# Second blocks of stick-breaking weights turned by VectorE, weights' low halves on GpSimd, v through DRAM, and the rotary product in another pool

## The chip, the cores and the metric

The kernel runs on one core of a Trainium2 chip. The metric is the device time of one execution in microseconds; lower is better. The time of a kernel is the median of several runs.

## The reference, cut to what matters

One layer of an encoder trunk over 1024 frames and 16 meta tokens (T = 1040 rows, 1024 features). `u` is the normalised input; one projection gives queries, keys, values and gates of two kinds of attention; both are gated and projected back.

```python
proj = jnp.einsum('bld,dc->blc', u, w_in)
sb_q, sb_k, sb_v, sb_g, df_q, df_k, df_v, df_g = jnp.split(proj, idx, axis=-1)

# stick-breaking attention: 8 heads of 64, strictly causal
z = einsum(q, k) * scale
log_beta = log_sigmoid(z)
log_keep = where(strict, log_sigmoid(-z), 0)
stick = reversed cumulative sum of log_keep
w = where(strict, exp(log_beta + stick), 0)
o = einsum(w, v)

# differential attention: 4 heads, rotary on q and k
p = softmax(where(mask, einsum(q, k) * scale, -1e30))
a = p[:, :, 0] - lam * p[:, :, 1]
o = rmsnorm(einsum(a, v), subln_g) * (1 - lambda_init)

mix = concat([sb_o * silu(sb_g), df_o * silu(df_g)])
h = h + einsum(mix, w_out);  y = rmsnorm(h, final_norm_gain)
```

## The kernel before

The sequence is stored in reverse, so a query block b of 128 rows sees the keys from its own place to the end: NB - b key tiles and 16 remaining columns. Work is cut into eight groups. Groups 0 to 3 are stick-breaking, two heads each (`sb_attention`); groups 4 to 7 are differential, one head each (`df_steps`). `build` puts the attention of group gi beside the projection of group gi + 1 with `weave`, which advances whichever of the two generators is behind by estimated TensorE time; the last two groups are woven with the output projection. What `weave` emits is then put in order for each engine by the framework's planner, which uses estimated durations (TC_OPTS, L922). Each engine runs its own queue strictly in that order. All DMAs that matter here are issued from SyncE's queue, also in order.

A projection unit (`proj`, L162) is one of v, q, k, g of a group: its weights come in two halves by `w_half` (L140). Each half is loaded into `wraw` (two buffers), rounded by ScalarE to a high part `wh` (L146), and VectorE subtracts for the low part `wl` (L147); `wh` and `wl` have three buffers each. Three matmuls (L157 to L159) use high times high, high times low and low times high, into one of two PSUM banks "mm". `ORDER` (L912) lists the units of each group: for groups 1 to 6 q, v, the remainder of v (r), k, g.

`sb_weights` (L512) makes the weights of one block of one head: scores on TensorE (L508, L509), a mask on VectorE (L520), two sigmoids on ScalarE (L521, L522), a running product on VectorE (scan, L525), and a multiplication (L527); a corner of it is copied by GpSimd (L528). `sb_transpose` (L531) turns it one step later, tile by tile of 128 keys. For even blocks of four tiles or more (8, 6 and 4 tiles, blocks 0, 2 and 4), as long as the rotary tables are not loaded, `turn` (L251) does it: VectorE transposes 32x32 squares into a spare tile (the buffers of the rotary tables `cosr` and `sinr`, two in all), four DMAs write that to DRAM (L260), and one DMA loads it back into place (L262). All other blocks go through TensorE (L551) and ScalarE (L552). `sb_pv` (L556) multiplies a pair of blocks with v (L574). `df_constants` loads the rotary tables when q of group 4 begins, at the start of project(4), which runs beside the attention of group 3; so group 3 uses TensorE alone.

`make_v` (L264) turns v of groups 1 to 6: VectorE transposes 32x32 squares, and 16 DMAs of 32 KB move them into place (L283). `evac_rope` (L202) empties PSUM for the rotary q and k: a product with the cosine (L209), two half products with the sine into a tile `t2` (L211) from the pool `a4` (tag "be", four buffers, that the attention uses for its weights), and an add on GpSimd (L212). The pool `tp` (tag "t", three buffers) holds the projections' results, the low part of q and v's turned tile.

Of the kernel before, what the change touches and what calls it, by code (L numbers as in the profile page):

```python
# [19 lines left out]
F32 = mybir.dt.float32  # L20
# [5 lines left out]
P = 128  # L26
D = 1024
SEQ = 1024
NMETA = 16
T = SEQ + NMETA  # L30
NB = SEQ // P
# [12 lines left out]
def chunks(width):  # L44
    if width <= 512:
        return [(0, width)]
    if width <= 1024:
        h = (width // 4) * 2
        return [(0, h), (h, width - h)]
    return list(CH_K)  # L50


class Build:
    def __init__(self, tc, es, i, out, mix_dram, turn_dram):
        self.tc, self.nc, self.es, self.i = tc, tc.nc, es, i
        self.out, self.mix_dram, self.turn_dram = out, mix_dram, turn_dram
        self.n = 0

        self.nu, self.rotary = 0, False

    def name(self, s):
        self.n += 1
# [77 lines left out]
    def w_half(self, u, h, copy=None, room=None):  # L140

        nc = self.nc
        raw = self.tl(self.wp2, [P, 4, P], F32, "wraw")
        nc.sync.dma_start(out=raw, in_=self.i["w_in"][u, :, 4 * h:4 * h + 4, :])
        hi, lo = room or (self.tl(self.wp3, [P, 4, P], F32R, n) for n in ("wh", "wl"))
        (copy or nc.scalar.copy)(out=hi, in_=raw)  # L146
        nc.vector.tensor_sub(lo, raw, hi.bitcast(F32))  # L147
        return hi, lo

    def mm3(self, ps, w, kt, c0, cn):  # L150
# [51 lines left out]
    def evac_rope(self, t):  # L202

        nc = self.nc

        def post(ps, c0, cn):
            s = slice(c0, c0 + cn)
            t2 = self.tl(self.a4, [P, T], F32, "be")
            nc.vector.tensor_mul(t[:, s], ps[:, :cn], self.cosr[:, s])  # L209
            for a, b in ((0, 64), (64, 0)):  # L210
                nc.vector.tensor_mul(t2[a:a + 64, :cn], ps[b:b + 64, :cn], self.sinr[a:a + 64, s])  # L211
            nc.gpsimd.tensor_add(t[:, s], t[:, s], t2[:, :cn])  # L212
        return post
# [34 lines left out]
                self.move(a[r + n:r + 2 * n], a[r:r + n])  # L248
        st["kh"], st["kl"] = (ha, hb), (la, lb)

    def turn(self, u, src, dst):  # L251


        nc = self.nc
        n = src.shape[1] // P
        nc.vector.transpose(out=u[:, :n * P].rearrange("p (m t r) -> p t m r", m=4, r=32),
                            in_=src.rearrange("p (t m r) -> p t m r", m=4, r=32))
        d = self.turn_dram[self.nu % 4]
        for a in range(4):
            nc.sync.dma_start(out=d[:, a, :n * 32].rearrange("(m k) c -> k m c", k=32),  # L260
                              in_=u[32 * a:32 * a + 32, :n * P].rearrange("k (m c) -> k m c", m=4))
        nc.sync.dma_start(out=dst, in_=d[:, :, :n * 32].rearrange("p a (t r) -> p a t r", r=32))  # L262

    def make_v(self, t, st, sb, on_pe):  # L264


        nc = self.nc
        v = self.tl(self.a2, [P, NB, P], F32, "v")
        off = NMETA if sb else 0
        if on_pe:  # L270
            for j0 in range(0, NB, 4):
                tr = self.bank("tr")
                for j in range(4):
                    c = off + P * (j0 + j)
                    nc.tensor.transpose(tr[:, j * P:(j + 1) * P], t[:, c:c + P], self.ident)
                nc.scalar.copy(out=v[:, j0:j0 + 4, :], in_=tr)
        else:
            u = self.tl(self.tp, [P, T], F32, "t")[:, :SEQ]
            nc.vector.transpose(out=u, in_=t[:, off:off + SEQ])
            u = u.rearrange("p (t j r) -> p t j r", j=4, r=32)  # L280
            for a in range(0, P, 32):
                for j in range(4):
                    nc.sync.dma_start(out=v[32 * j:32 * j + 32, :, a:a + 32], in_=u[a:a + 32, :, j, :])  # L283
        st["v"] = v
        if sb:
            tc_ = self.tl(self.a3, [P, P], F32, "on")
            nc.gpsimd.tensor_copy(tc_.rearrange("p (b c) -> p b c", c=16),
                                  t[:, :SEQ].rearrange("p (b c) -> p b c", c=P)[:, :, :16])
            st["vrt"] = tc_
        else:  # L290
            st["vrt"] = t[:, SEQ:T]
# [50 lines left out]
    def project(self, gi, st, first=False):  # L342
# [33 lines left out]
        parts = {"v": v, "r": vr, "q": q, "k": k, "g": g}  # L376
        for part in (parts[c] for c in ("vr" if first else ORDER[gi])):
            yield from part()
# [133 lines left out]
    def sb_weights(self, st, hd, b):  # L512
        nc = self.nc
        kw = T - b * P
        beta = self.tl(self.a4, [P, T], F32, "be")
        keep = self.tl(self.a4, [P, T], F32, "be")
        for c0, cn in chunks(kw):
            z = self.qk(st, hd, b, c0, cn)
            if c0 == 0:
                nc.vector.tensor_add(z[:, :P], z[:, :P], self.zmask)  # L520
            nc.scalar.activation(keep[:, c0:c0 + cn], z[:, :cn], AF.Sigmoid, scale=-1.0)  # L521
            nc.scalar.activation(beta[:, c0:c0 + cn], z[:, :cn], AF.Sigmoid)  # L522
            yield 2 * cn * MM_NS
        yield SB_PAD
        nc.vector.tensor_tensor_scan(out=keep[:, :kw], data0=keep[:, :kw], data1=self.zero.to_broadcast([P, kw]),  # L525
                                     initial=1.0, op0=ALU.mult, op1=ALU.add)
        nc.vector.tensor_mul(beta[:, 1:kw], beta[:, 1:kw], keep[:, :kw - 1])  # L527
        nc.gpsimd.tensor_copy(st["wrem"][32 * hd:32 * hd + 16, b], beta[:16, :16])  # L528
        st["w", hd, b] = beta

    def sb_transpose(self, st, hd, b):  # L531

        nc = self.nc
        n = NB - b
        e = b % 2
        w = st.pop(("w", hd, b))
        if e == 0:
            wt = self.tl(self.a2, [P, 2 * NB * P], F32, "wt")
            st["wt", hd] = wt.rearrange("p (e a j r) -> p e a j r", e=2, a=4, r=32)
        wt = st["wt", hd][:, e]  # L540
        if e == 0 and n >= SB_TURN and not self.rotary:
            self.nu += 1
            u = self.tl(self.const, [P, T], F32, ("cosr", "sinr")[self.nu % 2])
            self.turn(u, w[:, NMETA:NMETA + n * P], wt[:, :, e:e + n])
            return
        for m0 in range(0, n, 4):
            mn = min(4, n - m0)
            tr = self.bank("tr")
            for m in range(mn):
                c = NMETA + P * (m0 + m)  # L550
                nc.tensor.transpose(tr[:, m * P:(m + 1) * P], w[:, c:c + P], self.ident)  # L551
            nc.scalar.copy(out=wt[:, :, m0 + e:m0 + e + mn].rearrange("p a m r -> p m a r"),  # L552
                           in_=tr[:, :mn * P].rearrange("p (m a r) -> p m a r", a=4, r=32))
            yield mn * 110
# [354 lines left out]
END_PAD = 3000  # L909
LEAD, CUT, CUT_NS = 5, 8, 22e3  # L910

ORDER = [""] + 6 * ["qvrkg"] + ["qkvrg"]  # L912

SB_TURN = 4

AHEAD = 3
LAST_CUT = [(0, 512), (512, 256), (768, 256)]
# [61 lines left out]
```

## Time and profile before

| | |
|---|---|
| Median of 3 runs | 689.79 us (686.61 to 689.93) |
| The profiled execution | 689.24 us |
| Its span, first to last instruction | 687.4 us |
| TensorE busy | 663.5 us, 97% of the span |
| VectorE busy | 513.2 us, 75% |
| ScalarE busy | 350.8 us, 51% |
| GpSimd busy | 137.0 us, 20% |
| TensorE clock granted, mean | 0.987 |

Busy time is a share of one execution. Matmuls are pipelined and their ends are modelled, so that a busy TensorE can still run below its peak. An engine's idle time is put down to what came last before it went on. PE is TensorE, PEld its weight loads, DVE is VectorE, ACT ScalarE, POOL GpSimd and SPq the queue of SyncE, which issues the DMAs.

### The profile page before, as it was taken

What the parts mean: (1) busy time and instruction counts of PE and PEld (TensorE: products, weight loads), DVE (VectorE), ACT (ScalarE), POOL (GpSimd) and SP (SyncE); (2) the same over time, 40 slices, a digit from 0 to 9 for tenths busy, and PEclk for the clock granted to TensorE, in tenths of its full rate; (3) what the DMA queues carried; (4) which work ended last, traced back from release to release, by engine and by line L of the source; (5) the groups of instructions that cost most, each with busy time, mean ns of one, the idle gap of its engine ahead of it and who ended that gap; (6) DMA issues with size and microseconds to landing.
All of it is one profiled execution on the core that took longest, in us unless ns stands there. A gap on an engine that the chain in (4) does not pass through costs nothing.

```text
span 687.4 us, 11400 instructions
## 1 busy us (share of the span) xinstructions
PE 663.5 (97%) x3908; PEld 577.5 (84%) x3908; DVE 513.2 (75%) x1053; ACT 350.8 (51%) x931; POOL 137.0 (20%) x188
## 2 busy tenths in 40 slices
PE   8999999999979998989999999999999999999996
PEld 7888998798858996779878998899889987888785
DVE  6744998699829985698858785878589687776653
ACT  6513545545534552565544656555655436655642
POOL 0030021122210112040411022202222053011222
PEclk9999999999989999999999999999999999999998
DMA  8215647374645658022352324042504772122322
GB/s 327 93 33 140 171 124 188 87 218 121 144 118 138 165 112 239 16 77 55 72 123 62 74 67 124 32 117 53 124 32 101 201 239 87 63 84 77 105 92 92
DMA packets 76617, 78.83 MB, mean 115 GB/s; under 512 B 32528, under 2 KB 56208, under 8 KB 76560
## 3 DMA queue, kind: packets, MB, share of 16 engines
q1 hardware_dynamic: 76416, 78.10, 41.6%
q8 instruction: 31, 0.51, 0.3%
q14 instruction: 26, 0.21, 0.1%
q10 hardware_dynamic: 144, 0.00, 0.0%
HBM read 41.44 MB, written 14.42 MB: 81 GB/s over the span
## 4 chain that ended last, share of the span: by engine, by line
PE 71%; DVE 10%; DMA 8%; issue 3%; ACT 3%; SPq 3%; POOL 1%; POOLq 0%; DVEq 0%; ACTq 0%
PE mm L157 12%; PE mm L158 12%; PE mm L159 12%; PE mm L756 10%; PE pv L694 4%; PE z L508 4%; PE z L509 4%; PE pv L574 3%; DVE be L525 2%; PE tr L677 2%; DMA wt<-turn_scratch 2%; PE tr L551 2%; DVE be L527 1%; DMA hb<-ha 1%; SPq L283 1%
## 5 line engine op out<-in xcount | busy, mean ns | idle before, releaser
L157 PE MATMUL mm<-xh,wh 128*128 128x346 f32 (+2 forms) x592 | 211.6, 358 | 2.6 <-DVE be L211 2.2
L158 PE MATMUL mm<-xl,wh 128*128 128x346 f32 (+2 forms) x592 | 210.9, 356 | 0.0
L159 PE MATMUL mm<-xh,wl 128*128 128x346 f32 (+2 forms) x592 | 209.9, 355 | 0.0
L157 PEld LDWEIGHTS mm<-xh,wh 128*128 128x128 f32 x592 | 112.3, 190 | 13.3 <-DVE be L211 2.5
L159 PEld LDWEIGHTS mm<-xh,wl 128*128 128x128 f32 x592 | 112.1, 189 | 9.1 <-issue 0.5
L158 PEld LDWEIGHTS mm<-xl,wh 128*128 128x128 f32 x592 | 112.2, 189 | 8.5 <-issue 0.7
L525 DVE TENSOR_TENSOR_SCAN be<-be,zero 128x1040 f32<-128x1040 f32 (+7 forms) x64 | 92.2, 1446 | 16.5 <-ACT be L521 16.4
L521 ACT ACTIVATE be<-z 128x456 f32<-128x456 f32 (+8 forms) x112 | 49.8, 458 | 86.7 <-DVE z L520 51.2
L643 ACT ACTIVATE be<-z,nm 128x346 f32<-128x346 f32 (+8 forms) x112 | 59.9, 540 | 50.4 <-DVE nm L640 34.6
L528 POOL COPY rem<-be 16x16 f32<-16x16 f32 x64 | 34.6, 540 | 192.0 <-DVE be L527 177.0
L633 DVE TENSOR_REDUCE nm<-z 128x1 f32<-128x346 f32 (+8 forms) x112 | 54.6, 502 | 4.7 <-PE z L509 3.6
L522 ACT ACTIVATE be<-z 128x346 f32<-128x346 f32 (+8 forms) x112 | 48.6, 464 | 13.3 <-DVE be L527 12.1
L146 ACT CAST wh<-wraw 128x512 fp32r<-128x512 f32 x58 | 36.2, 626 | 36.6 <-PE mm L158 27.2
L527 DVE TENSOR_TENSOR be<-be,be 128x1039 f32<-128x1039 f32 (+7 forms) x64 | 49.2, 769 | 4.0 <-ACT be L522 0.9
L147 DVE TENSOR_TENSOR wl<-wraw,wh 128x512 fp32r<-128x512 f32 x58 | 40.0, 691 | 10.3 <-ACT wh L146 9.7
L702 POOL TENSOR_TENSOR rr<-rr,mhalf 128x1 f32<-128x1 f32 x32 | 19.7, 616 | 137.8 <-DVE rr L701 98.9
L508 PE MATMUL z<-ha,qa 128*128 128x346 f32 (+8 forms) x112 | 37.9, 344 | 4.2 <-DMA ha<-ha 1.9
L574 PE MATMUL pv<-wt,v 128*64 128x256 f32 (+1 forms) x336 | 37.4, 368 | 4.6 <-DMA wt<-turn_scratch 4.6
L508 PE MATMUL z<-hb,qb 128*128 128x346 f32 (+8 forms) x112 | 38.2, 341 | 0.6 <-ACT be L522 0.3
L552 ACT COPY wt<-tr 128x512 f32<-128x512 f32 (+3 forms) x66 | 28.7, 461 | 19.1 <-PE pv L574 9.5
L694 PEld LDWEIGHTS pv<-v,wt 128*128 128x128 f32 x288 | 36.8, 191 | 1.8
L694 PE MATMUL pv<-v,wt 128*128 128x128 f32 x288 | 38.2, 275 | 0.0
(237 smaller groups left out, 1220.1 us busy)
## 6 DMA issues: line engine op xcount, KB each, us to landing
wraw<-w_in SPq DMA_DIRECT2D x58, 256.0 KB, 3.0
t<-w_out SPq DMA_DIRECT2D x8, 512.0 KB, 4.3
wt<-turn_scratch SPq DMA_DIRECT2D x6, 512.0 KB, 4.4
v<-t SPq DMA_DIRECT2D x96, 32.0 KB, 2.0
mix_scratch<-gate SPq DMA_DIRECT2D x6, 512.0 KB, 4.0
t<-mix_scratch SPq DMA_DIRECT2D x16, 192.0 KB, 2.5
wt<-turn_scratch SPq DMA_DIRECT2D x6, 384.0 KB, 4.2
hb<-ha SPq DMA_DIRECT2D x8, 260.0 KB, 3.9
```

Of the source, the lines that this page charges most:

```text
L157: nc.tensor.matmul(o, hi[:, k, :], xh, start=kt == 0, stop=False)
L158: nc.tensor.matmul(o, hi[:, k, :], xl, start=False, stop=False)
L159: nc.tensor.matmul(o, lo[:, k, :], xh, start=False, stop=kt == KT - 1)
L508: nc.tensor.matmul(z[:, :cn], q, st["kh"][hd][:, s], start=True, stop=False)
L521: nc.scalar.activation(keep[:, c0:c0 + cn], z[:, :cn], AF.Sigmoid, scale=-1.0)
L525: nc.vector.tensor_tensor_scan(out=keep[:, :kw], data0=keep[:, :kw], data1=self.zero.to_broadcast([P, kw]), initial=1.0, op0=ALU.mult, op1 ...
L527: nc.vector.tensor_mul(beta[:, 1:kw], beta[:, 1:kw], keep[:, :kw - 1])
L574: nc.tensor.matmul(pv[r, s], st["v"][:, b + j, r], w, start=p in ends[0], stop=p in ends[1])
L633: nc.vector.tensor_reduce(out=nm[:, comp, j:j + 1], in_=z[:, :cn], op=ALU.max, axis=AX.X, negate=True)
L643: nc.scalar.activation(p[:, c0:c0 + cn], zs[j][:, :cn], AF.Exp, bias=bias, accum_out=sm[:, comp, j:j + 1])
L694: nc.tensor.matmul(po[:, :P], wt[:, m, :], st["v"][:, b + m, :], start=m == 0, stop=False)
L756: self.nc.tensor.matmul(ps[:, :cn], a, b[kt][:, w], start=first and n == 0, stop=last and n == 2)
```

## The change

- `w_half`: the low half of the weights is subtracted by GpSimd instead of VectorE.
- `evac_rope`: the tile `t2` comes from the pool `tp` instead of `a4`.
- `turn` only transposes and writes to DRAM, and returns a function that loads. The first part now runs at the end of `sb_weights`, the load in `sb_transpose`.
- `SB_TURN` is a pair: even blocks of four tiles or more are turned in this way, and now odd blocks of five or more too (7 and 5 tiles, blocks 1 and 3). Eight places in DRAM are used in turn instead of four.
- `make_v`: the 16 direct DMAs become `turn` with four writes and four loads.
- `ORDER`: group 4 projects g first, then q, v, r, k.

```diff
@@ w_half
-        nc.vector.tensor_sub(lo, raw, hi.bitcast(F32))
+        nc.gpsimd.tensor_sub(lo, raw, hi.bitcast(F32))
@@ evac_rope
-            t2 = self.tl(self.a4, [P, T], F32, "be")
+            t2 = self.tl(self.tp, [P, T], F32, "t")
@@ turn
-    def turn(self, u, src, dst):
+    def turn(self, u, src):
...
-        d = self.turn_dram[self.nu % 4]
+        self.nd += 1
+        d = self.turn_dram[self.nd % 8]
         for a in range(4):
             nc.sync.dma_start(out=d[:, a, :n * 32].rearrange("(m k) c -> k m c", k=32),
                               in_=u[32 * a:32 * a + 32, :n * P].rearrange("k (m c) -> k m c", m=4))
-        nc.sync.dma_start(out=dst, in_=d[:, :, :n * 32].rearrange("p a (t r) -> p a t r", r=32))
+        back = d[:, :, :n * 32].rearrange("p a (t r) -> p a t r", r=32)
+
+        def load(dst, by_a=False):
+            for a in (range(4) if by_a else [slice(0, 4)]):
+                nc.sync.dma_start(out=dst[:, a], in_=back[:, a])
+        return load
@@ make_v
-            nc.vector.transpose(out=u, in_=t[:, off:off + SEQ])
-            u = u.rearrange("p (t j r) -> p t j r", j=4, r=32)
-            for a in range(0, P, 32):
-                for j in range(4):
-                    nc.sync.dma_start(out=v[32 * j:32 * j + 32, :, a:a + 32], in_=u[a:a + 32, :, j, :])
+            self.turn(u, t[:, off:off + SEQ])(v.rearrange("p t (a r) -> p a t r", a=4), by_a=True)
@@ sb_weights, at its end
-        st["w", hd, b] = beta
+        n = NB - b
+        if n >= SB_TURN[b % 2] and not self.rotary:
+            self.nu += 1
+            u = self.tl(self.const, [P, T], F32, ("cosr", "sinr")[self.nu % 2])
+            st["w", hd, b] = self.turn(u, beta[:, NMETA:NMETA + n * P])
+        else:
+            st["w", hd, b] = beta
@@ sb_transpose
-        if e == 0 and n >= SB_TURN and not self.rotary:
-            self.nu += 1
-            u = self.tl(self.const, [P, T], F32, ("cosr", "sinr")[self.nu % 2])
-            self.turn(u, w[:, NMETA:NMETA + n * P], wt[:, :, e:e + n])
+        if callable(w):
+            w(wt[:, :, e:e + n])
             return
@@
-ORDER = [""] + 6 * ["qvrkg"] + ["qkvrg"]
+ORDER = [""] + 3 * ["qvrkg"] + ["gqvrk"] + 2 * ["qvrkg"] + ["qkvrg"]
-SB_TURN = 4
+SB_TURN = 4, 5
```

## Rows read from the trace of the kernel before

**Rows 1.** The page, busy us (share of the span) and instructions of each engine.
```profile
PE 663.5 (97%) x3908; PEld 577.5 (84%) x3908; DVE 513.2 (75%) x1053; ACT 350.8 (51%) x931; POOL 137.0 (20%) x188
```
**Rows 2.** Windows: stretch, length, busy us of PE, PEld, DVE, ACT, POOL; clock, DMA.
```profile
60.00:364.00 304.00, 292.62 (x1762) 249.14 (x1761) 240.56 (x351) 148.40 (x356) 58.24 (x88) 0.98 0.49 125
364.00:560.00 196.00, 193.69 (x1212) 177.95 (x1211) 151.75 (x412) 109.89 (x334) 40.69 (x50) 1.00 0.37 97
```
**Rows 3.** Waits from 60 to 364 us: total us, times, longest us.
```profile
PE pv L574 <- DMA wt<-turn_scratch: 4.6, 2, 4.4
...
PE mm L157 <- DVE be L211: 2.2, 1, 2.2
...
PE z L508 <- DMA ha<-ha: 1.9, 1, 1.9
```
**Rows 4.** Windows at the lower clock (the column behind POOL is the granted clock).
```profile
191.40:198.20 6.80, 4.92 (x21) 3.21 (x22) 0.72 (x2) 0.70 (x3) 0.00 (x0) 0.50 0.59 140
...
273.30:276.70 3.40, 3.40 (x15) 2.73 (x16) 0.30 (x1) 1.07 (x4) 0.83 (x1) 0.50 0.55 180
...
304.00:307.40 3.40, 3.40 (x15) 3.33 (x14) 3.29 (x3) 1.96 (x4) 2.32 (x2) 0.51 0.11 25
```
**Rows 5.** Timeline of all engines from 100 us: start us, us, instruction.
```profile
103.58 0.62 PEld L551 LDWEIGHTS tr<-ident,be 128*128 128x128 f32 x5
...
104.17 0.19 PEld L159 LDWEIGHTS mm<-xh,wl 128*128 128x128 f32 x1
```
**Rows 6.** Groups by line and shape: count | busy us, mean ns | idle before.
```profile
L147 DVE TENSOR_TENSOR wl<-wraw,wh 128x512 fp32r<-128x512 f32 x58 | 40.0, 691 | 10.3 <-ACT wh L146 9.7 <-PE pv L697 0.3
...
L551 PE MATMUL tr<-ident,be 128*128 128x128 f32 x180 | 29.1, 277 | 1.5 <-DVE be L527 1.5
...
L325 POOL TENSOR_TENSOR gate<-gate,be 128x512 f32<-128x512 f32 x16 | 21.3, 1342 | 31.4 <-ACT be L322 26.6 <-DVE cc L653 4.3 <-POOL rem L528 0.6
...
L256 DVE STREAM_TRANSPOSE sinr<-be 128x1024 f32<-128x1024 f32 x3 | 3.7, 1243 | 0.1
...
L256 DVE STREAM_TRANSPOSE sinr<-be 128x768 f32<-128x768 f32 x3 | 2.9, 975 | 0.1
```
**Rows 7.** Timeline of SyncE's queue, group 1.
```profile
175.18 3.89 SPq L283 DMA_DIRECT2D v<-t  x6
179.16 2.00 SPq L260 DMA_DIRECT2D turn_scratch<-sinr  x4
```
**Rows 8.** Instructions of L260 (first two rows), and of L262 (last).
```profile
L260 SPq DMA_DIRECT2D turn_scratch<-sinr x36: 319/446/791, 70.6 to 253.2; - x36
...
DMA to landing us min/median/max: 1.8/2.4/5.2
...
DMA to landing us min/median/max: 3.2/4.3/7.0
```
**Rows 9.** The chain that ended last, in order of time: start us, us.
```profile
94.23 3.39 PE pv L574 x32
```
**Rows 10.** Timeline of VectorE, group 0.
```profile
86.17 1.10 DVE L527 TENSOR_TENSOR be<-be,be 128x911 f32<-128x911 f32 x1
```
**Rows 11.** Timeline of VectorE, group 3.
```profile
293.75 2.93 DVE L525 TENSOR_TENSOR_SCAN be<-be,zero 128x912 f32<-128x912 f32 x1
```
**Rows 12.** Timeline of GpSimd, group 3.
```profile
293.47 1.30 POOL L212 TENSOR_TENSOR t<-t,be 128x512 f32<-128x512 f32 x1 [1.29 <-DVE be L211]
```
**Rows 13.** Timeline of VectorE, group 1.
```profile
151.29 2.04 DVE L525 TENSOR_TENSOR_SCAN be<-be,zero 128x912 f32<-128x912 f32 x1
...
157.46 0.68 DVE L147 TENSOR_TENSOR wl<-wraw,wh 128x512 fp32r<-128x512 f32 x1
```
**Rows 14.** Timeline of TensorE, group 1.
```profile
159.68 0.32 PE L159 MATMUL mm<-xh,wl 128*128 128x348 f32 x1
```
**Rows 15.** Timeline of SyncE's queue, keys of group 4.
```profile
342.46 3.58 SPq L216 DMA_DIRECT2D hb<-ha  x4
...
351.00 1.76 SPq L216 DMA_DIRECT2D la<-la  x2
```

More of the change, by code (lines that the diff above doesn't have):

```diff
@@ L57, in __init__ @@
         self.n = 0
-        self.nu, self.rotary = 0, False
+        self.nu, self.nd, self.rotary = 0, 0, False
     def name(self, s):
@@ L972 @@
     mix_dram = nc.dram_tensor("mix_scratch", (NB, P, KT, P), F32, kind="Internal").ap()
-    turn_dram = nc.dram_tensor("turn_scratch", (4, P, 4, NB * 32), F32, kind="Internal").ap()
+    turn_dram = nc.dram_tensor("turn_scratch", (8, P, 4, NB * 32), F32, kind="Internal").ap()
     with tile.TileContext(nc, **TC_OPTS) as tc:
```

## The prediction

> **What bounds the kernel now.** I read the page's busy line first, then windows by stage, then TensorE's waits, then the timelines of VectorE, GpSimd and the DMA queue. TensorE is busy 97% of the span [rows 1]. The stage that the change touches, the four stick-breaking groups with their projections, runs from about 60 to 364 us; TensorE is busy there for 292.6 of 304 us, VectorE for 240.6 [rows 2]. So TensorE sets the end, with VectorE not far behind: in the middle of a group VectorE's timeline has hardly a gap. In the differential groups from 364 to 560 us TensorE is idle for 2.3 us in all [rows 2], so nothing that frees VectorE can give much there.
>
> TensorE's idle time in the first stage is small and sits in three places: 4.4 us before the products of a pair, waiting for turned weights from DRAM; 1.9 us before scores, waiting for the keys' moves; 2.2 us before projection matmuls, where a rotary product holds the PSUM bank [rows 3]. Each is followed by a stretch at the lower of the clock's two levels: 0.50 granted (1.2 GHz) in 6.8, 3.4 and 3.4 us [rows 4]. Work that ran there took twice its time, so these cost 4.92/2 = 2.5, 1.7 and 1.7 us more.
>
> The execution took 689.24 us, 1.8 us more than its span of 687.4, and 0.55 us less than the median of the runs, 689.79. The sum is made against 689.24. About 0.5% (3.4 us) is the least change that a measurement of this kernel can tell from none.
>
> **The change, part by part.**
>
> *Second blocks turned by VectorE.* Per head of groups 0 to 2 the blocks of 7 and 5 key tiles leave TensorE: 12 transposes, 72 in six heads. For group 3, g now comes first in project(4), so the rotary tables come later. With the weave's numbers (g is 10.2 of 43 units of projection, so attention has come to 25.7 of 108, and a block's weights cost about 5.8) the blocks 0 and 1 of both heads are ready and block 2 is not: 2 x (8 + 7) = 30 transposes more. 102 of the 180 go. Five took 0.59 us of TensorE's weight loading (103.58 until the next load at 104.17) [rows 5], 0.118 each; I take 0.115: **-11.7 us**. Bounds: 0, if TensorE had time to spare where they stood, and -102 x 0.162 = -16.5 from the group's mean, 29.1 us for 180 [rows 6].
>
> VectorE pays: a transpose of 8 tiles takes 1.24 us, of 6 tiles 0.975 [rows 6], 0.13 a tile, so 1.11 for 7 and 0.84 for 5: 6 x 1.95 + 2 x (1.24 + 1.11) = 16.4 us.
>
> *Turned data sooner for even blocks.* The transpose and the writes now follow the weights at once, and the load comes a step later, when the writes have landed. The pair with the 4.4 us wait had its first writes issued at 179.16, behind six of v's small transfers that held the queue from 175.18 to 179.07 [rows 7]. Both causes get smaller. At best 4.4 + 2.5 + 0.2 = -7.1; at worst 0. I take **-5**.
>
> *Odd blocks get a DMA in their way.* This is the cost that I know least. The chain is transpose 1.1, four writes at 0.446, landing 2.4, load issue about 0.4, landing 4.3 [rows 6, 8]: 10.0 us. In the kernel before, the products of blocks 0 and 1 begin 94.23 - 87.27 = 7.0 us after the odd block's last multiplication [rows 9, 10]. If TensorE's queue kept that order, each such pair would wait 3.0 us. There are seven (two pairs in groups 0 to 2, one in group 3). But the order of TensorE's queue is planned from estimated ends of the transfers, so the products move back behind projection matmuls, of which there are enough in mid-group. What is left is the planner's error. The pairs whose two even blocks came last by DMA before waited 4.4 us and twice 0.2 or less [rows 3]: 1.5 on average, at the end of a group, where little else is left to run. In mid-group I take 1.0: **+7**. Bounds: 0 and 7 x (3.0 + 2.5) = +39, each wait with a clock drop as dear as the first in [rows 4].
>
> *Weights' low halves on GpSimd.* VectorE loses 58 x 0.69 = 40.0 us [rows 6], 32 of them in the first stage. GpSimd takes 1.34 us for an operation of that shape [rows 6], so 78 us on an engine that is busy 137. VectorE's scan and a GpSimd operation with two inputs keep each other out: a 912-wide scan took 2.93 us beside the rotary add of 1.30 us, and 2.04 alone [rows 11 to 13]. A low half that meets a scan or the multiplication thus costs VectorE up to 0.9 us, against 0.69 saved; I assume that half meet one, so VectorE is helped little in the first stage. TensorE needs the half later: the tightest ended at 158.14 and was used at 159.68 [rows 13, 14], 1.5 us of slack; on GpSimd 0.65 less, and less again by a scan if it has to wait for one. Behind a low half that waits on GpSimd stand the rotary adds and the small powers of the differential groups. I take **+1**; bounds -3, if VectorE's relief shortens waits, and +29 x 1.1 = +32, if every second half came late by a scan's 2.0 minus the remaining 0.9.
>
> The Trainium skill (GPSIMD Engine Reference, "Engine selection" and "Specifications") advises VectorE for elementwise work on a tile, with GpSimd about 2x slower for two inputs and sharing its SBUF interfaces with VectorE instructions that have two SBUF inputs. The trace agrees, 1.34 against 0.69 and 2.93 against 2.04. By that rule the move is a loss, which is the third rival below.
>
> *v by way of DRAM.* Sixteen issues at 0.65 us [rows 7] become eight; 48 issues less in six groups are 31 us of the DMA queue. The new turned blocks add 64 writes and 16 loads, about 36 us. v's loads wait for its writes to land (2.4 us), with weight loads and key moves queued behind. v is first read one attention later, some 70 us, and that hides it; without that cover it would be late by 2.4 + 4.3 us. **0**, bounds -2 and +6 x 2.4 = +14.
>
> *g first in project(4).* Then k is last before the differential groups. Its twelve moves took from 342.46 to 352.76 [rows 15], and g's matmuls covered them; now only q of the next group can. The border one group earlier, where moves came late, cost the 1.9 us wait in [rows 3]. **+1.5**; bounds 0 and +10.3, nothing covered. At that earlier border the queue holds fewer v issues and no rotary tables now, but more turns: of 1.9 + 1.7 I take back **-1.5**; bounds -3.6 and +3.6.
>
> *Rotary product in the other pool.* It no longer waits for the attention's four buffers, but shares three with t, the low part of q and v's turned tile. **0**; bounds -3.9, if the 2.2 us wait and its clock drop go, and +26, 20 chunks by an add of 1.3 [rows 12].
>
> Sum: -11.7 - 5 + 7 + 1 + 0 + 1.5 - 1.5 + 0 = -8.7, so 689.24 - 8.7 = **680.5 us**.
>
> **The rivals.** *First, the forecast:* TensorE's saved transposes stay saved, 680.5, its own range 670 to 686. For it: 96% busy in the stage [rows 2]. Against: VectorE at 79%.
>
> *Second, no change to be told:* the waits move from even to odd blocks and eat what the transposes give. With 7 waits of 2.2 us instead of 1.0 the sum is about 0: 689.
>
> *Third, GpSimd's lock:* VectorE stops for 0.9 us at each of 32 low halves, +29, saves 22 and gains 16.4 of transposes: 24 us more on 240.6. That alone would still fit into 304 us; it decides once the scans run so late that the products wait. If half of it shows, and the transposes give nothing in that state, 689.2 + 12 - 5 = 696.
>
> *Fourth, slower by the odd blocks:* if TensorE's queue reaches the products less than 10.0 us after the multiplication, seven waits of 3.0 and, at four of them, a clock drop of 2.5 come to 31 instead of 7: 680.5 + 24 = 704. VectorE would join it if writes stayed queued behind v as at 175.18: there are two turn tiles, and scans stand behind the third turn.
>
> **How the numbers follow.** Forecast 0.60, second rival 0.14, third 0.12, fourth 0.14. The forecast is faster by 1.3%, so faster 0.60, within 0.5% 0.14, slower 0.26. Eight in ten: 668 (the unknown terms at their better bounds, all but two) to 698 (the third rival and the milder half of the fourth).
>
> **What would show it.** 78 transposes of stick-breaking weights instead of 180. No wait of TensorE for turned weights at the last pair with four tiles; waits for them at the pairs with 8 and 6 tiles are the new cost, and over 2 us each with clock drops would make the fourth rival true. Scans well over their 2.04 us beside the low halves speak for the third. A wait of projection matmuls for GpSimd would show low halves late; a wait of scores for key moves at group 4's start would show the price of the new order. I am wrong above all if the planner's transfers are much faster than the chip's.

## Result and profile after

The changed kernel takes 723.89 us (median of 4 runs, 717.86 to 726.58) where the kernel before takes 689.39 us beside it: a ratio of 1.048, with a 95% interval of 1.043 to 1.052. The forecast was 680.5 us, with a range up to 698. The time went the other way, and lies above the slowest rival (704).

The profiled execution took 717.86 us, the fastest of the four; its rows explain 28.6 of the 34.5 us between the medians. The page's busy line, to be held against [rows 1]:

```profile
PE 661.3 (92%) x3806; PEld 574.9 (80%) x3806; DVE 507.0 (71%) x1011; ACT 337.5 (47%) x899; POOL 202.3 (28%) x246
```

The span grew from 687.4 to 716.1 us. TensorE is idle for 716.1 - 661.3 = 54.8 us against 23.9, 30.9 more, and busy for 2.2 less. The work left it as announced, and the time did not. VectorE is less busy than before, so no engine has become the bound by its sum of work.

The windows of [rows 2], and the two behind them (stretch, length, busy us of PE, PEld, DVE, ACT, POOL, granted clock, DMA share, GB/s):

```profile
60.00:364.00 304.00, 272.11 (x1589) 233.38 (x1588) 241.40 (x319) 130.23 (x312) 87.29 (x117) 0.97 0.63 168
364.00:560.00 196.00, 190.94 (x1135) 172.87 (x1134) 124.57 (x337) 94.93 (x279) 60.12 (x62) 0.99 0.37 94
...
560.00:640.00 80.00, 72.54 (x420) 61.38 (x419) 62.28 (x176) 48.43 (x155) 22.03 (x29) 0.98 0.36 119
640.00:716.00 76.00, 68.44 (x367) 57.02 (x365) 44.80 (x132) 37.49 (x121) 17.11 (x21) 0.99 0.24 85
```

In the stick-breaking stage TensorE is idle for 31.9 us instead of 11.4, and the DMA engines' share rises from 0.49 to 0.63. Then the idle time stays small until 560 us, and from 560 to 640 there are 7.5 us, where the kernel before had 1.2:

```profile
560.00:640.00 80.00, 78.85 (x431) 66.39 (x430) 61.94 (x185) 47.09 (x155) 19.95 (x26) 1.00 0.31 102
```

TensorE's waits from 60 to 364 us, against [rows 3] (total us, times, longest us):

```profile
PE pv L581 <- DMA wt<-turn_scratch: 9.4, 5, 3.1
PE z L511 <- ACT be L525: 5.9, 4, 4.3
PE pv L581 <- DMA turn_scratch<-sinr: 5.0, 1, 5.0
PE mm L157 <- DVE gate L320: 3.6, 1, 3.6
PE mm L159 <- POOL wl L147: 2.4, 1, 2.4
```

Products wait for turned data for 14.4 us instead of 4.6. The other half of the added 20.5 us is spread over waits for ScalarE, VectorE and one low half. Two waits near 4 us, at 300 and 320 us, each go with a stretch at the lower clock, as in [rows 4]:

```profile
301.40:308.20 6.80, 4.09 (x10) 3.22 (x11) 6.27 (x7) 3.17 (x7) 2.56 (x3) 0.50 0.73 208
321.90:328.70 6.80, 4.71 (x22) 3.36 (x24) 5.82 (x8) 5.06 (x9) 1.46 (x2) 0.50 0.36 133
```

Two groups of [rows 6] by line and shape (count, busy us, mean ns, idle before):

```profile
L147 POOL TENSOR_TENSOR wl<-wraw,wh 128x512 fp32r<-128x512 f32 x58 | 84.8, 1464 | 140.3 <-ACT wh L146 124.9 <-DMA turn_scratch<-sinr 10.1 <-DMA lb<-la 1.6
...
L558 PE MATMUL tr<-ident,be 128*128 128x128 f32 x78 | 13.9, 278 | 1.7 <-DVE be L530 1.7
```

78 transposes are left of 180, and the low halves cost 1.46 us each on GpSimd. The odd block's way to the products of the first pair, on VectorE's timeline, SyncE's queue and TensorE's timeline (start us, us):

```profile
86.31 1.09 DVE L530 TENSOR_TENSOR be<-be,be 128x911 f32<-128x911 f32 x1
...
90.26 1.06 DVE L257 STREAM_TRANSPOSE cosr<-be 128x896 f32<-128x896 f32 x1
```
```profile
90.78 1.62 SPq L262 DMA_DIRECT2D turn_scratch<-t  x3
92.44 2.17 SPq L262 DMA_DIRECT2D turn_scratch<-cosr  x4
94.66 0.45 SPq L262 DMA_DIRECT2D turn_scratch<-t  x1
95.21 1.85 SPq L262 DMA_DIRECT2D turn_scratch<-sinr  x4
97.17 0.55 SPq L268 DMA_DIRECT2D wt<-turn_scratch  x1
```
```profile
101.36 3.55 PE L581 MATMUL pv<-wt,v 128*64 128x256 f32 x32
```

The multiplication ends at 87.40 and the products begin at 101.36, 14.0 us later, where it was 7.0 before [rows 9, 10] and I had reckoned with 10.0. The transpose starts 2.9 us late, v's writes stand on both sides of its four writes, and its load stands behind the next block's writes.

### The profile page after: what moved, and what is told of

Same layout as the page of the kernel before. It is cut to its first block, busy times and chain, and to the rows that moved or that the text cites. A ratio compares the mean times of both kernels' runs of the same rounds, so it can differ in the third digit from the quotient of the medians.

```text
span 716.1 us, 11271 instructions
## 1 busy us (share of the span) xinstructions
PE 661.3 (92%) x3806; PEld 574.9 (80%) x3806; DVE 507.0 (71%) x1011; ACT 337.5 (47%) x899; POOL 202.3 (28%) x246
## 4 chain that ended last, share of the span: by engine, by line
PE 56%; DMA 15%; DVE 15%; ACT 5%; SPq 4%; issue 4%; POOL 1%; DVEq 0%; POOLq 0%; ACTq 0%
PE mm L763 10%; PE mm L157 9%; PE mm L159 9%; PE mm L158 9%; PE pv L581 4%; DMA turn_scratch<-cosr 3%; DVE be L528 3%; PE pv L701 3%; PE z L511 3%; SPq L262 3%; PE z L512 3%; DVE be L530 2%; DMA turn_scratch<-sinr 2%; DMA wt<-turn_scratch 2%; DMA lb<-la 1%
## 5 line engine op out<-in xcount | busy, mean ns | idle before, releaser
L147 POOL TENSOR_TENSOR wl<-wraw,wh 128x512 fp32r<-128x512 f32 x58 | 84.8, 1464 | 140.3 <-ACT wh L146 124.9
L528 DVE TENSOR_TENSOR_SCAN be<-be,zero 128x1040 f32<-128x1040 f32 (+7 forms) x64 | 95.3, 1494 | 21.7 <-ACT be L524 21.1
L524 ACT ACTIVATE be<-z 128x346 f32<-128x346 f32 (+8 forms) x112 | 50.3, 458 | 96.8 <-DVE z L523 64.5
L530 DVE TENSOR_TENSOR be<-be,be 128x1039 f32<-128x1039 f32 (+7 forms) x64 | 57.2, 893 | 7.1 <-ACT be L525 4.6
L640 DVE TENSOR_REDUCE nm<-z 128x1 f32<-128x346 f32 (+8 forms) x112 | 54.2, 498 | 10.3 <-PE z L512 9.6
L525 ACT ACTIVATE be<-z 128x346 f32<-128x346 f32 (+8 forms) x112 | 48.8, 460 | 21.8 <-DVE be L530 9.5
L531 POOL COPY rem<-be 16x16 f32<-16x16 f32 x64 | 21.0, 328 | 122.4 <-DVE be L530 122.0
L581 PE MATMUL pv<-wt,v 128*64 128x256 f32 (+1 forms) x336 | 40.8, 390 | 14.7 <-DMA wt<-turn_scratch 9.4
L581 PEld LDWEIGHTS pv<-wt,v 128*64 128x64 f32 x336 | 29.4, 152 | 24.8 <-issue 19.0
L709 POOL TENSOR_TENSOR rr<-rr,mhalf 128x1 f32<-128x1 f32 x32 | 21.5, 670 | 95.3 <-DVE rr L708 86.9
L511 PE MATMUL z<-ha,qa 128*128 128x346 f32 (+8 forms) x112 | 38.0, 346 | 6.8 <-ACT be L525 4.9
L511 PE MATMUL z<-hb,qb 128*128 128x346 f32 (+8 forms) x112 | 37.8, 339 | 2.6 <-ACT be L650 1.6
```

The lines of the kernel that those rows point to most:

```text
L147: nc.gpsimd.tensor_sub(lo, raw, hi.bitcast(F32))
L511: nc.tensor.matmul(z[:, :cn], q, st["kh"][hd][:, s], start=True, stop=False)
L581: nc.tensor.matmul(pv[r, s], st["v"][:, b + j, r], w, start=p in ends[0], stop=p in ends[1])
L640: nc.vector.tensor_reduce(out=nm[:, comp, j:j + 1], in_=z[:, :cn], op=ALU.max, axis=AX.X, negate=True)
```

## The experiments

Each kernel was timed beside the kernel before. Nearly all the edits undo one part of the diff or do it alone. Ratios are to the kernel before; 1% is 6.9 us.

**A path from before to after, one part at a time** (each kernel is the one above it with one more part):

| kernel | ratio (95%) | step |
|---|---|---|
| before | 1 | |
| even blocks' turn at once | 0.9951 (0.9928 to 0.9975) | -0.5% |
| and v by way of DRAM | 0.9960 (0.9942 to 0.9977) | +0.1% |
| and the rotary product in the other pool | 1.0032 (1.0009 to 1.0055) | +0.7% |
| and low halves on GpSimd | 1.0084 (1.0054 to 1.0115) | +0.5% |
| and g first, k last in project(4) | 1.0123 (1.0076 to 1.0170) | +0.4% |
| and odd blocks turned: the changed kernel | 1.0478 (1.0434 to 1.0521) | +3.5% |

Steps below some 0.5% are within the intervals. The last one is not: some 24 us for the odd blocks, although 86 transposes go with them (from 164 to 78; the new order had already taken the 16 of group 3's first blocks). The parts aren't additive, though, as the runs below show.

**Parts undone in the changed kernel.** First the order, then the low halves, then the odd blocks:

```diff
-ORDER = [""] + 3 * ["qvrkg"] + ["gqvrk"] + 2 * ["qvrkg"] + ["qkvrg"]
+ORDER = [""] + 6 * ["qvrkg"] + ["qkvrg"]
```


> The changed kernel with group 4's units in the old order (q, v, r, k, g). Theory A (k last before the differential groups costs most): their attention starts about 28 us sooner again, and the time falls by 15 to 25 us, to 700 to 708. Theory B (low halves on GpSimd): falls by under 5 us, to 719 or more. Theory C (odd blocks' transfers): by under 5 us too; group 3 then turns nothing, which takes one late pair away.

Measured 702.12 us, 1.0174 (1.0123 to 1.0226): 3.0% of the 4.8% come back by the order alone. (Group 3's turned blocks go with it, since the rotary tables come early again; a run below shows that these blocks cost nothing.)

```diff
-        nc.gpsimd.tensor_sub(lo, raw, hi.bitcast(F32))
+        nc.vector.tensor_sub(lo, raw, hi.bitcast(F32))
```


> The changed kernel with the weights' low halves on VectorE again. Theory B: GpSimd's queue holds low halves behind waits (the trace shows 125 us of waiting for ScalarE's high halves there, and the DMA queue 135 us behind low halves), so the time falls by 15 to 25 us, to 700 to 708. Theory A and theory C: falls by under 6 us, to 718 or more.

720.4 us, 1.0443 (1.0388 to 1.0498): not told apart from the changed kernel. GpSimd's part is not what makes this kernel slow.

```diff
-SB_TURN = 4, 5
+SB_TURN = 4, 99
```


> The changed kernel with odd blocks on TensorE again, even blocks still turned early. Theory C: the six waits of products for turned weights, 14.4 us together, and their clock drops go; the time falls by 12 to 20 us, to 704 to 712. Theory A and theory B: TensorE's 78 transposes come back (+9 us) against the waits, so within 6 us of 724.

698.67 us, 1.0123 (1.0076 to 1.0170): 3.5% come back. Order and odd blocks give back 3.0 and 3.5 of 4.8, so part of the loss needs both.

**The order alone, in the kernel before** (the first diff of this section reversed):

> The kernel before with only group 4's units in the new order (g first, k last). Theory A: slower by 15 to 25 us, 704 to 714. Theories B and C: within 5 us of 689, because the weight halves and the turned blocks stay as they were, apart from group 3's even blocks.

703.21 us, 1.0209 (1.0147 to 1.0271), so it costs 2.1% by itself. SyncE's queue, TensorE's timeline and a window of this run:

```profile
340.28 11.16 SPq L283 DMA_DIRECT2D v<-t  x16
351.54 4.44 SPq L144 DMA_DIRECT2D wraw<-w_in  x2
357.39 2.46 SPq L216 DMA_DIRECT2D hb<-ha  x4
```
```profile
369.34 0.72 PE L509 MATMUL z<-la,qa 128*128 128x348 f32 x3 [1.89 <-DMA la<-la]
372.22 0.66 PE L508 MATMUL z<-hb,qb 128*128 128x348 f32 x1 [2.16 <-ACT be L643]
```
```profile
370.00:380.00 10.00, 6.36 (x20) 5.64 (x20) 7.65 (x19) 3.41 (x12) 1.28 (x1) 0.56 0.20 62
```

The key moves begin at 357.39, 15 us later than in [rows 15]; TensorE waits for one of them, then for ScalarE in the chain behind the scores, and the clock falls.

**The old order with other parts taken out of the changed kernel.** Even blocks alone turned; then low halves on VectorE as well; then, with low halves on GpSimd again, the rotary product's pool put back:

```diff
-ORDER = [""] + 3 * ["qvrkg"] + ["gqvrk"] + 2 * ["qvrkg"] + ["qkvrg"]
-SB_TURN = 4, 5
+ORDER = [""] + 6 * ["qvrkg"] + ["qkvrg"]
+SB_TURN = 4, 99
```


> The changed kernel without its new order and without odd blocks turned by VectorE; early turns of even blocks, v by way of DRAM, low halves on GpSimd and the rotary product in the other pool stay. If theories A and C act on their own, both gains add: 724 - 22 - 25 = 677 to 684. If the rest of the change (B, or the rotary product's pool) costs something in the differential groups, as their attention in the first two experiments' traces suggests, 686 to 697.

> The one before, with the weights' low halves on VectorE too. Theory B: faster than it by 5 us or more, because GpSimd's small powers no longer stand behind low halves that wait for ScalarE. Rival: within 3 us of it, since low halves were seen 0.1 us or more before use, with one exception.

```diff
-            t2 = self.tl(self.tp, [P, T], F32, "t")
+            t2 = self.tl(self.a4, [P, T], F32, "be")
```


> The first one, with the rotary product in the attention's pool again. If the pool is what slows the differential groups: faster than the first by 5 us or more. Rival: within 3 us.

696.1, 691.91 and 698.32 us: 1.0084, 1.0032 and 1.0096 (1.0063 to 1.0128). The odd blocks cost only 0.9% here (from 1.0084 to the 1.0174 of the old order with them); the low halves 0.5%; the pool nothing that can be told.

**Low halves alone, in the kernel before** (the second diff of this section reversed):

> The kernel before with only the low halves on GpSimd. Theory B: slower by 5 to 12 us, 695 to 702, most of it behind 364 us. Rival (the relief of VectorE is worth as much as the waits cost): within 3.4 us of 689.

702.56 us, 1.0172 (1.0146 to 1.0198). VectorE's scans and multiplications of the stick-breaking weights, all shapes together, in the kernel before and then in this run:

```profile
L525 DVE TENSOR_TENSOR_SCAN be<-be,zero 128x1040 f32<-128x1040 f32 (+7 forms) x64 | 92.2, 1446 | 16.5 <-ACT be L521 16.4
L527 DVE TENSOR_TENSOR be<-be,be 128x1039 f32<-128x1039 f32 (+7 forms) x64 | 49.2, 769 | 4.0 <-ACT be L522 0.9
```
```profile
L525 DVE TENSOR_TENSOR_SCAN be<-be,zero 128x1040 f32<-128x1040 f32 (+7 forms) x64 | 94.5, 1478 | 21.4 <-ACT be L521 21.2
L527 DVE TENSOR_TENSOR be<-be,be 128x1039 f32<-128x1039 f32 (+7 forms) x64 | 59.0, 921 | 4.5 <-ACT be L522 0.4
```

The multiplications take 9.8 us more and the scans 2.3 us (the 912-wide ones 2318 ns on average instead of 2157, the 1040-wide ones no more than before). The same move lengthens the two by 11.8 us from the kernel at 1.0032 above to the one at 1.0084, and by 14.2 us from the changed kernel with low halves on VectorE to the changed kernel. TensorE's matmuls never wait for a low half in this run; its transposes wait 3.7 us for multiplications instead of 1.5, and its products 7.6 us for turned weights instead of 4.6. The loss is real. That the longer multiplications cause it is not shown: they are lengthened as much between those two kernels, where the low halves cost only 0.5%.

**Is it the rotary tables, which odd turns of group 3 displace?** The changed kernel with no turned block in group 3:

```diff
-        if n >= SB_TURN[b % 2] and not self.rotary:
+        if n >= SB_TURN[b % 2] and not self.rotary and st["turns"]:
...
-            nxt = {}
+            nxt = {"turns": gi < 2}
```


> The changed kernel, but group 3 turns no block by VectorE (groups 0 to 2 as changed, new order kept). Theory D (the two turn tiles are the rotary tables' buffers, so that turning both blocks of group 3 lets the tables and the lambda vectors arrive in mid-attention and stops VectorE's queue): the 19 us that order and odd blocks cost together beyond their single costs go, 703 to 708. Rival (the new order and the late pairs of groups 0 to 2 do it without group 3): 718 or more.

722.14 us, 1.0463 (1.0441 to 1.0484): no change. This theory fell.

**Parts that could win, alone in the kernel before**: even blocks' transpose and writes at once, the load a step later; then the odd blocks too; then only v by way of DRAM:

```diff
+        if n >= SB_TURN[b % 2] and not self.rotary:
...
+            st["w", hd, b] = self.turn(u, beta[:, NMETA:NMETA + n * P])
...
-SB_TURN = 4
+SB_TURN = 4, 99
```


> The kernel before with only the early transposes and writes of even blocks (load one step later). If the stall of 4.4 us and its clock drop go for good: faster by 3 to 7 us, 683 to 687. Rival (what is gained in the stick-breaking groups is given back in the last groups, as in the experiment with low halves on VectorE): within 3.4 us of 690.

```diff
-SB_TURN = 4, 99
+SB_TURN = 4, 5
```


> The one before with odd blocks of 7 and 5 tiles turned as well, nothing else of the change. Theory C: slower than it by 5 to 10 us, products waiting 10 us or more in all for turned weights. Rival (the transposes' 8 us count): faster than it by 3 us or more.

```diff
-            for a in range(0, P, 32):
-                for j in range(4):
-                    nc.sync.dma_start(out=v[32 * j:32 * j + 32, :, a:a + 32], in_=u[a:a + 32, :, j, :])
+            self.turn(u, t[:, off:off + SEQ], v.rearrange("p t (a r) -> p a t r", a=4), by_a=True)
```


> The kernel before with only v turned by way of DRAM. My term of the sum was 0, bounds -2 and +14: within 3.4 us of 690. Rival: slower by 4 us or more, the queue waiting for v's writes to land.

687.05 us, 0.9951 (0.9928 to 0.9975); 710.77 us, 1.0303 (1.0282 to 1.0324); 687.74 us, 0.9967 (0.9940 to 0.9995). So the odd blocks cost 3.5% on nothing but early even blocks, old order and VectorE's low halves included. 18.4 of the 22.7 us between the two spans are TensorE's idle time from 60 to 310 us, 29.7 us instead of 11.3 (early even blocks, then with the odd ones):

```profile
60.00:310.00 250.00, 238.65 (x1451) 204.32 (x1452) 204.13 (x287) 123.93 (x295) 46.42 (x72) 0.99 0.55 138
```
```profile
60.00:310.00 250.00, 220.30 (x1248) 183.29 (x1246) 188.65 (x269) 100.09 (x240) 32.62 (x63) 0.96 0.66 168
```

There the products wait for turned data no longer than before. From 60 to 310 us, TensorE's, then ScalarE's waits with the odd blocks, and SyncE's queue from 180 us:

```profile
PE z L515 <- DMA ha<-ha: 5.0, 1, 5.0
PE pv L585 <- DMA wt<-turn_scratch: 4.0, 1, 4.0
```
```profile
ACT wh L146 <- DMA wraw<-w_in: 23.0, 6, 7.3
```
```profile
182.75 2.01 SPq L262 DMA_DIRECT2D turn_scratch<-cosr  x4
184.86 2.19 SPq L268 DMA_DIRECT2D wt<-turn_scratch  x1
187.10 7.99 SPq L290 DMA_DIRECT2D v<-t  x12
195.19 2.00 SPq L262 DMA_DIRECT2D turn_scratch<-sinr  x4
197.24 0.58 SPq L268 DMA_DIRECT2D wt<-turn_scratch  x1
197.91 2.04 SPq L262 DMA_DIRECT2D turn_scratch<-cosr  x4
200.06 1.30 SPq L216 DMA_DIRECT2D hb<-ha  x2
```

ScalarE waits 23.0 us for raw weights, where the kernel with early even blocks alone has 2.8. The queue has no gap in this stretch: turns, v, key moves and weights stand in one line, and what is late is the projection's weights and the next keys, whose moves begin at 200.06 us, where early even blocks alone have them at 183.29. Is that the queue, or VectorE's 12 us of transposes and its two turn tiles? Four runs were made to tell:

f1 is even blocks at once and v by way of DRAM (both edits above), f2 is f1 with `SB_TURN = 4, 5`. f3 is early even blocks, with the odd ones transposed by VectorE into the turn tiles and the result thrown away, while TensorE transposes them as well:

```diff
-            st["w", hd, b] = self.turn(u, beta[:, NMETA:NMETA + n * P])
+            load = self.turn(u, beta[:, NMETA:NMETA + n * P], b % 2)
+            st["w", hd, b] = beta if b % 2 else load
```

f4 is early even blocks and odd blocks, whose four writes are issued by GpSimd:

```diff
-            nc.sync.dma_start(out=d[:, a, :n * 32].rearrange("(m k) c -> k m c", k=32),
+            q.dma_start(out=d[:, a, :n * 32].rearrange("(m k) c -> k m c", k=32),
...
-            st["w", hd, b] = self.turn(u, beta[:, NMETA:NMETA + n * P])
+            st["w", hd, b] = self.turn(u, beta[:, NMETA:NMETA + n * P], (nc.sync, nc.gpsimd)[b % 2])
```


> Kernel before with the two parts that were faster alone: even blocks' transpose and writes at once with the load a step later (-2.8 us alone) and v by way of DRAM (-2.1 us alone). If the two remove different waits they add: 689.4 - 4.9 = 684.5. If both remove the same wait (the writes of a turned block behind v's sixteen small transfers in SyncE's queue) the second gives nothing: 687.

> The run before with the second blocks of 7 and 5 key tiles turned as well. Queue theory (C1): the odd blocks cost 24 us on early even blocks alone because their writes and loads stand with v's sixteen issues in SyncE's queue and push weights and key moves back; with eight issues for v instead of sixteen the cost falls to about half, some 697. VectorE theory (C2): the cost is VectorE's added transposes and its stops for the two turn tiles, which v's transfers do not touch: 684.5 + 22 = 706 or more.

> Even blocks early as before, and VectorE also makes the transposes of the blocks of 7 and 5 key tiles into the turn tiles, but nothing of that is written to DRAM or used: TensorE still transposes those blocks. So VectorE pays the whole price, the DMA queue none, and TensorE saves nothing. C2 (VectorE's time): slower by much of the 24 us, 700 or above. C1 (the queue): little slower than the 687 of early even blocks alone, 687 to 692.

> Even blocks early and odd blocks turned (710.8 us when every transfer goes through SyncE's queue), with the odd blocks' four writes issued on GpSimd's queue instead. C1: a good part of the 24 us comes back, 695 to 700, unless GpSimd's own issue makes the writes land later. C2: no change, 708 to 712.

Then g1: f2 with the odd blocks' writes and loads both on GpSimd's queue (the edit of f4 and this one):

```diff
-                nc.sync.dma_start(out=dst[:, a], in_=back[:, a])
+                q.dma_start(out=dst[:, a], in_=back[:, a])
```


> Early even blocks and v by way of DRAM (687.6 us) with the odd blocks turned, and the odd blocks' four writes and their load all issued on GpSimd's queue, so that SyncE's queue holds fewer issues than in the kernel before. With the writes alone moved, the load still stood in SyncE's queue and waited there 13.1 us for writes to land. C1, if the queue is the whole cost: no more than 688, and down to 680 if the 72 saved transposes count. If something else of the odd blocks costs too (VectorE stops 11.9 us for the turn tiles in the run with all on SyncE): 694 to 700.

| odd blocks | on | ratio (95%) | over its base | ScalarE waits for weights, 60 to 310 us |
|---|---|---|---|---|
| not turned | early even | 0.9951 | | 2.8 |
| turned, all by SyncE | early even | 1.0303 (1.0282 to 1.0324) | +3.5% | 23.0 |
| transposed, unused (f3) | early even | 0.9999 (0.9978 to 1.0021) | +0.5% | 11.3 |
| writes by GpSimd (f4) | early even | 1.0184 (1.0148 to 1.0219) | +2.3% | 22.9 |
| not turned (f1) | and v by DRAM | 0.9960 | | none |
| turned, all by SyncE (f2) | and v by DRAM | 1.0152 (1.0118 to 1.0185) | +1.9% | 10.7 |
| writes and loads by GpSimd (g1) | and v by DRAM | 1.0121 (1.0081 to 1.0162) | +1.6% | 1.6 |

VectorE's added transposes are the small part, 0.5%. Relieving SyncE's queue takes off more: eight issues less for each v take the cost from 3.5 to 1.9%, and moving 48 writes takes it to 2.3%. With the whole round trip elsewhere the weights are in time, and 1.6% remain, which can't be told from f2's 1.9%. So the queue is shown for about half of the cost. ScalarE's wait for weights marks a full queue, but its length isn't the price: f3 has 11.3 us of it and loses 0.5%, and f4 has as much as the kernel with all by SyncE, since its loads stand in that queue until GpSimd's writes have landed. In f4 TensorE itself waits 11.1 us for rounded weights, with all by SyncE 2.3 us.

Two rivals for the rest were not tried apart. VectorE stops for the two turn tiles, which f3 leaves out: 14.6 us in f2, 9.6 in g1 and none in f1, but none in f4 either. And the transfers themselves: the DMA engines' busy share from 60 to 310 us is 0.66 to 0.67 in all four kernels with turned odd blocks, whichever queue issues them, and 0.53 to 0.55 in f1, f3 and early even blocks alone; raw weights land after 3.6 to 4.1 us (median) instead of 3.0 to 3.4. g1's windows against f1's, 60 to 310 us:

```profile
60.00:310.00 250.00, 228.72 (x1324) 196.37 (x1323) 205.63 (x290) 110.84 (x260) 76.49 (x129) 0.97 0.66 178
```
```profile
60.00:310.00 250.00, 239.12 (x1442) 203.84 (x1442) 203.33 (x283) 124.01 (x293) 36.95 (x71) 0.99 0.55 143
```

TensorE's idle time in this stretch grows from 10.9 to 21.3 us, more than the 8.3 us that 72 transposes at 0.115 took, and the clock is 0.97 instead of 0.99, worth 2% of 229 = 4.6 us. 10.4 + 4.6 - 8.3 = 6.7 of the 8.5 us between the two spans (693.9 and 685.4). Products wait directly for turned data 6.4 us in either run, so it is not that wait that grew; what the added idle time is due to, g1 does not show. f1 also answers the other question: the two parts that won alone do not add (0.9960).

**A control**: the kernel before with one number of the weave changed, the same instructions in another order:

```diff
-SB_PAD, DF_PAD = 5000, 3000
+SB_PAD, DF_PAD = 5500, 3000
```


> A control: the kernel before with the same instructions and one number of the weave changed (the cost put in for a score chunk's pad, 5500 instead of 5000), so that only the order in which attention and projection are planned shifts, in some 1,600 lines of TensorE's order. If reorderings alone move the time by little, within 0.5%, the single-part runs measure their parts. If it moves by 1% or more, the 13 us of the new order and of the low halves alone may be the planner's luck and not the part's price.

688.73 us, 1.0007 (0.9983 to 1.0031). This reordering by itself moves nothing, which speaks against the larger prices above being just another order. One control doesn't exclude it, least of all for steps of half a per cent.

**Why order and odd blocks need each other.** With the new order the odd blocks cost 3.5%, with the old one 0.9% (both with low halves on GpSimd). The rows that differ are the key moves of group 4, SyncE's queue of the changed kernel:

```profile
350.97 1.91 SPq L262 DMA_DIRECT2D turn_scratch<-t  x4
353.95 2.67 SPq L268 DMA_DIRECT2D v<-turn_scratch  x4
...
369.20 2.43 SPq L216 DMA_DIRECT2D hb<-ha  x4
...
374.01 1.86 SPq L216 DMA_DIRECT2D lb<-la  x3
```

and of the same kernel with the old order:

```profile
347.92 2.42 SPq L216 DMA_DIRECT2D hb<-ha  x4
```

Windows of one of the two matmul lines of a score, the one with the keys' high part (L511; length, TensorE's busy us with it, clock), the changed kernel:

```profile
360.00:380.00 20.00, 0.00 (x0) 1.00 0.47 117
380.00:400.00 20.00, 2.71 (x9) 1.00 0.53 143
...
560.00:640.00 80.00, 12.06 (x35) 0.98 0.36 119
640.00:716.00 76.00, 3.07 (x11) 0.99 0.24 85
```

and the old order:

```profile
360.00:380.00 20.00, 2.51 (x8) 1.00 0.14 41
```

In the kernel before these moves begin at 342.46 [rows 15]. Odd blocks with the old order put them at 347.92, the new order without odd blocks at 349.41, the order alone, behind v's sixteen issues, at 357.39, and both together at 369.20. For 20 us no score runs. TensorE isn't idle then: it does projection ahead of its turn. The projections run out shortly after 560 us. The scores left over, 3.07 us of this line behind 640 where the kernel before has none, are computed in the tail, with only the output's matmuls to fill the gaps, and from 560 to 640 there are 7.5 us of idle time. That the late scores cause these is not shown: the longest wait there, 2.5 us, is that of an output matmul for GpSimd (L191).

Idle time of TensorE by stretch, us (length of the windows less TensorE's busy time), shows how much is paid where:

| kernel | 60 to 310 | 310 to 364 | 364 to 560 | 560 to 640 | 640 to the end |
|---|---|---|---|---|---|
| before | 11.4 | 0.0 | 2.3 | 1.2 | 6.8 |
| order alone | 13.3 | 2.3 | 8.2 | 2.5 | 7.5 |
| changed, without odd blocks | 7.9 | 1.8 | 6.9 | 4.0 | 8.1 |
| changed, with the old order | 21.5 | 1.8 | 1.6 | 2.8 | 7.3 |
| changed | 27.3 | 4.6 | 5.1 | 7.5 | 7.7 |

The odd blocks are paid where they are turned: 19.4 of the 24.0 us that they add to the changed kernel's idle time lie before 310 us. The order alone is paid mostly as soon as the late keys are needed, 8.2 of 12.7 us between 310 and 560. Beside the odd blocks it adds 17.7 us in all, 5.8 before 310 and 4.7 from 560 to 640; so late keys paid at the end are at most a part of it. Why the delays more than add up isn't settled by this; that group 3's own turned blocks are not the reason, the run without them shows.

## Why the prediction was wrong

- **The step that failed is the odd blocks' DMA, +7 us.** They cost some 24 us in the changed kernel with what their transposes gave back, and up to 10 more if the 86 transposes gave their 0.115 us each; the bound was +39, and it was meant for another way. I priced direct waits of products and let the planner move them back. It did, as the pair at 101.36 shows, and direct waits grew by only 10 us (14.4 against 4.6), near the +7 that I gave them. What I left out is that 64 writes and 16 loads stand in the same in-order queue as the weights and keys. I had counted them, 36 us of the queue against 31 released, and called the difference nothing. f2 and f4 show the price of the queue: less of v's issues or of the odd writes in it, and 1.2 to 1.6% come back. g1 shows that it isn't the whole: 1.6% stay, and their cause is open.
- **The transposes' -11.7 us was not realised.** All 102 went, their busy time fell from 29.1 to 13.9 us, and TensorE's busy sum by 2.2 us only. The lower mean clock (0.980 against 0.987, about 5 us of 716) takes back a part; what took back the rest is open. The bound of 0, "if TensorE had time to spare", is nearer: in g1 more idle time came up than was saved. I read 96% busy as "TensorE sets the end". That the attention's chain sets the pace, with projection as its filler, fits the scores' windows in part; it was not tried apart.
- **k last, +1.5 us with a bound of +10.3, failed too.** It costs 0.4% on top of one set of parts, 2.1% alone and 3.0% beside the odd blocks. The bound counted the time of the moves themselves. What it left out is that the moves begin 15 us later, behind v's issues, and the waits and the lower clock that follow when the next attention starts late: alone, the order adds 12.7 us of idle time, 5.9 of it from 364 to 560 us.
- **Low halves, +1 us**: 0.5% (3.6 us) on the path, within noise in the changed kernel (0.3%), and 1.7% (11.9 us) alone. The term was too small. Its mark did appear, on multiplications more than on scans: VectorE loses 12 to 14 us by it, where half of the stage's 32 low halves at 0.9 us make 14.4. (The scan of 2.04 us [rows 13] that I called alone stood beside a GpSimd copy.) The longest wait of the changed kernel for a low half is one of 2.4 us. The Trainium skill (GPSIMD Engine Reference, "Engine selection") speaks for VectorE, at about half the time; 1.46 us against 0.69 agrees. VectorE's operations are lengthened as much on the path as alone, so why the loss is small there and large here stays open.
- **Even blocks sooner, -5 us**: -3.4 us measured, but not as forecast. Products still wait 5.3 us for turned data (4.6 before), and TensorE's idle time from 60 to 310 us is 11.3 us instead of 11.4. The longest such wait fell from 4.4 to 2.9 us, and the lower clock at 191 us is gone: the clock from 60 to 310 us is 0.99 instead of 0.97. That the number came near was partly luck. **v by way of DRAM, 0**: -2.3 us alone, nothing beside early even blocks; that both shorten the same stay behind v's sixteen issues is not shown. **The rotary product's pool, 0**: +0.7% with low halves on VectorE, nothing with them on GpSimd; this stays open.
- **The rivals**: the fourth was nearest in cause (odd blocks late, writes queued behind v, turn tiles), and too small, since it still priced only the products' waits. The second fell. The third had longer operations on VectorE right, at half their size, but the changed kernel with low halves on VectorE is as slow. The parts' costs do not add, so a sum of terms, each sized alone, misses what they cost together.

The best version is early even blocks alone (0.9951), which f1 equals: 0.5% faster than the kernel before. The gain hangs on neither the odd blocks, nor the order, nor GpSimd.

## What to carry to other kernels

When work is moved from a full engine to a DMA round trip, price the queue it is issued on: list what stands behind each added issue (weights, keys) and when that is due, and don't net issues added at one place against issues removed at another. On an engine kept busy by filler work, a late start of the dependent chain need not show as idle time at once, so read the windows of the chain's own instructions (here scores) over time, and not only the waits; and split each part's added idle time by stretch before saying where it is paid. Measure each part alone and on top of the others; here the low halves and the order cost 1.7 and 2.1% alone, the odd blocks 3.5% on early even ones, and all together 4.8%.

## What the runs showed of the hardware

With all 58 low halves on GpSimd and nothing else changed, VectorE's 64 multiplications of two tiles took 921 ns on average instead of 769, and its 64 scans 1478 instead of 1446; its maxima over the scores and its turns of weights, with one operand, took as long as before (502 ns, and 972 against 974 for `sinr`). In that run a low half that began at 294.54 us, beside a scan, took 2.52 us, where one at 279.04 took 1.27, and the 1039-wide multiplication that began beside it at 296.08 took 2.08 us, where one at 288.76 took 1.23.

Moving DMA issues to GpSimd's queue did not make them land sooner. The median time to landing there, g1's list of DMA issues (KB each, median us to landing), against 4.0 us and 4.5 us for the same two loads by SyncE in f2, which differs by the queue alone (loads of 384 KB, which stayed on SyncE's queue, landed later too, after 6.5 us instead of 4.7, so that GpSimd's queue is not shown to be the reason):

```profile
wt<-turn_scratch POOLq DMA_DIRECT2D x6, 448.0 KB, 5.4
...
wt<-turn_scratch POOLq DMA_DIRECT2D x6, 320.0 KB, 5.8
```
